# Narrower weight loads for the low products, and a later place for the first pair's far values

## The chip, the cores and the metric

The kernel runs on one core of a Trainium2 chip. The metric is the device time of one execution in microseconds (us); of a kernel that is run several times, the median counts.

## The reference: what is computed

One layer of a hybrid decoder on 1024 tokens of width 1024, all in float32:

```python
h = rmsnorm(x, mix_pre_norm[layer])
proj = h @ w_in[layer]
q_a, k_a, v_a, q_h, f_h, i_h, g_h = jnp.split(proj, splits, axis=-1)
...
attn = dilated_mixture_attention(q_a.reshape(ahead), k_a.reshape(ahead), v_a.reshape(ahead), slopes)
attn = rmsnorm(attn.reshape(B, S, ATTN_WIDTH), attn_out_norm[layer])
rec = hgrn2_recurrence(q_h, f_h, i_h, g_h, lower_bounds[layer], hgrn_out_norm[layer])
mixed = jnp.concatenate([attn, rec], axis=-1) @ w_out[layer]
x = x + rmsnorm(mixed, mix_post_norm[layer])
h = rmsnorm(x, mlp_pre_norm[layer])
ff = jnp.square(jax.nn.relu(h @ w_ff1[layer])) @ w_ff2[layer]
x = x + rmsnorm(ff, mlp_post_norm[layer])
```

The attention has 8 heads of 64 columns. Each query sees three sets of keys (a near window, every fourth token, every sixteenth token), and the three results are mixed by their softmax denominators. The recurrence (HGRN2) has 4 heads of 128 columns and is computed in blocks.

## The kernel before, in words

**Stages.** The core first does the 4 recurrence heads (`hgrn_core`), then the 8 attention heads in 4 pairs, then the output projection, then the feed-forward part, which is the longest (matrix products at line 2047 and lines 1602 to 1604). TensorE is fed in program order. Between the steps of a head a helper `fill` issues pieces of later projections from a queue, so that TensorE has work while the other engines prepare the next step. The projections of attention pairs 0 and 1 (`attn_proj(0)`, `attn_proj(1)`) are in this queue during the last recurrence head.

**High and low parts.** A product that must keep float32 precision is made of several products of rounded numbers: an operand is split into a high part (ScalarE rounds it, lines 86, 719, 993) and a low part (the rest, by VectorE or GpSimd). A projection is three products (`three_pass`, lines 90 to 92).

**Products with the values (`weigh`).** The values tile `v` holds for every block of 128 keys and each head of a pair 128 columns: 64 high columns and then 64 low columns. It is the stationary operand (its columns are the weight columns that are loaded), and the transposed probabilities are the moving operand. There are two products: the probabilities' high part (`pth`, `ptNh`, `ptFh`) and their low part (`ptl`, `ptNl`, `ptFl`). Both are accumulated into a PSUM tile of 128 rows, rows 0 to 63 for the high values and rows 64 to 127 for the low values, and later these halves are added (line 1062). Three kinds exist: D (line 1012; the diagonal part of a head, in two steps, 256 probabilities wide and at the last block 128 wide), F (line 1028, the far keys, 128 wide, three products for each of 4 classes), N (line 1034, the near window, 256 or 128 wide).

**Size-64 products of the recurrence.** At the end of each recurrence head 8 products of float32 numbers are made (line 583): the weights are 64 columns of `kt`, the moving operand is 64 columns of `qt`. Each appears in the profile as two matmuls, 64 of them in all 4 heads.

**Far values of pair 0.** The far products of pair 0 need the values in another order of rows. `values_turn` (line 756) makes the values tile and writes it to a buffer in HBM (`vd`, 8 DMAs at line 767); `far_load(0)` (line 665) makes two tiles `vf` in SBUF and fills them from there with 6 DMAs (line 672). All these DMAs are issued by SyncE (SP), which issues in program order. In the kernel before, `far_load(0)` is called at the end of the second `values_turn` of pair 0. Then follow on SP: the key copies of pair 0 (`kh`, `kl`; line 737: 4 and 4 DMAs from `hik` and `kf` for the first half of the tokens, 4 and 4 from `kp` for the second), with two weight loads (`raw`, line 107) among them; the first query copies of pair 1 (`q`, lines 798 and 799: 4 DMAs from `hiq` and `qf`); the second head's bias table (`bt`, line 855).

**What hangs on these copies.** `hiq`, `hik`, `qf`, `kf` share one pool of two buffers (`half`). VectorE makes `qf` out of the projection (line 793), ScalarE makes `hiq` from it (line 719), GpSimd makes the low part in place (line 720). The next `qf` needs a buffer whose copies by DMA have ended. Behind the second `qf` of pair 1 on VectorE stand the score steps of head 0 (line 901: add the bias and take the minimum). They empty the PSUM tiles `ps_D` and `ps_F`, of which there are two buffers, and the score products on TensorE (lines 896 and 897) and `px` (line 935) need these.

Of the kernel before, what the change touches and what calls it, by code (L numbers as in the profile page):

```python
# [17 lines left out]
P = 128  # L18
T = 1024
# [18 lines left out]
def hymba_layer(ctx, tc, x, w_in, w_out, w_ff1, w_ff2, g_pre, lb_logits, g_mix, g_post,  # L38
# [464 lines left out]
    def hgrn_core(h, after=None):  # L503
# [76 lines left out]
            fill(3500 if h < HH - 1 else (5300, 3100, 2000)[step])  # L580
        pl = bank("s", f"pl{h}_6")
        for n in range(NT):
            TE.matmul(pl[:64, n * 64:(n + 1) * 64], kt[:, n * P:n * P + 64], qt[:, n * P + 64:(n + 1) * P],
                      start=True, stop=True)
        S.activation(at[64:, :, 64:], at[64:, :, :64], AF.Copy)
        G.memset(at[64:, :, :64], 0.0)
# [75 lines left out]
    def key_blocks(ap, j0, j1):  # L662
        return ap.rearrange("p (r j i) -> p j r i", r=DIL, i=32)[:, j0:j1]

    def far_load(pr):
        fars[pr] = [slab("T", f"vf{pr}_{c}", F32R, (P, DIL, 2, 2, 64)) for c in range(2)]
        v2 = v_dram[pr].rearrange("(two odd) k c -> odd k two c", odd=2)
        for c in range(2):
            for odd in range(2):
                for c_, p0, k0, n in ((0, 0, 64 * odd, P), (1, 0, P - P * odd, 64), (1, 64, P - P * odd, 64)):  # L670
                    if c_ == c:
                        nc.sync.dma_start(out=f32(fars[pr][c][p0:p0 + n]).rearrange(
                            "p (two odd) h a d -> odd p two (h a d)", odd=2)[odd], in_=v2[odd, k0:k0 + n])
# [82 lines left out]
    def values_turn(tag="mm"):  # L756
        pr, vs, full, hf = turn_later.pop(0)
        pt = bank(tag, f"pvt{pr}{hf}")
        for j in range(4):
            TE.transpose(pt[:, j * P:(j + 1) * P], full[:, j * P:(j + 1) * P], ident)  # L760
        ptv = pt.rearrange("p (j h d) -> p j h d", j=4, h=2)
        dst = vs[:, hf * 4:hf * 4 + 4]
        S.activation(dst[:, :, :, 0, :], ptv, AF.Copy)
        V.tensor_tensor(out=dst[:, :, :, 1, :], in0=ptv, in1=f32(dst[:, :, :, 0, :]), op=ALU.subtract)
        b = slice(0, 4) if hf == 0 else slice(4, 6)
        for r in range(DIL):
            nc.sync.dma_start(out=v_dram[pr][r].rearrange("(n i) c -> i n c", i=32)[:, b],
                              in_=f32(vs[32 * r:32 * r + 32, b]).rearrange("p n h a d -> p n (h a d)"))
        if hf == 1 and pr == 0:
            far_load(0)  # L770

    def attn_proj(pr):
        stacks = [{}, {}]
# [4 lines left out]
        for hf in range(2):  # L778
# [17 lines left out]
            for i, (a, b) in enumerate(halves):  # L796
                c, d = halves[1 - i]
                nc.sync.dma_start(out=f32(stacks[i]["q"][a:b, sl]), in_=f32(hi[a:b]))
                nc.sync.dma_start(out=f32(stacks[i]["q"][c:d, sl]), in_=f32(lo[a:b]))
            yield 650.0  # L800
        wv = w_get(A0 + 3 * pr + 1, 0)
        vs = None
# [153 lines left out]
    def turn(hd, kind, g):  # L956
# [38 lines left out]
        if kind == "D" and g % 2 and hd // 2 < LASTP:  # L995
            V.reciprocal(st["rd"][:, g - 1:g + 1], st["dn"][:, g - 1:g + 1])

    def weigh(hd, kind, g):

        _, vs = pairs[hd // 2]  # L1000
# [4 lines left out]
        if kind == "D":  # L1005
# [3 lines left out]
            for j in range(nj):  # L1009
                c0 = P if j == nj - 1 else 0  # L1010
                for q in range(2):
                    TE.matmul(po[:, c0:256], v_of(vs, j), pt[q][:, j, c0:],  # L1012
                              start=j == 0 and q == 0, stop=j == nj - 1 and q == 1)
            ot = stats[hd]["D"][1] if g == 0 else stats[hd]["D"][3][:, :256]
            if hd // 2 == LASTP:
                S.activation(ot.rearrange("p (b i r) -> p b i r", b=2, r=DIL),
# [5 lines left out]
        if kind == "F":  # L1022
# [1 line left out]
                stats[hd]["po"] = bank("pv", f"pov{hd}_far")  # L1024
            po = stats[hd]["po"].rearrange("p (r m) -> p r m", r=DIL)
            for r in range(2 * g, 2 * g + 2):
                for n, (c, src) in enumerate(((0, pt[0][:, 0, r]), (0, pt[1][:, 0, r]), (1, pt[0][:, 1, r]))):
                    TE.matmul(po[:, r], v_of(fars[hd // 2][c], r), src, start=r == 0 and n == 0, stop=False,
                              skip_group_check=True)
            return None  # L1030
        po = stats[hd]["po"].rearrange("p (r m) -> p r m", r=DIL)
        for j, s0, n, c0 in (((3, 0, 1, 0), (4, 1, 2, 0)), ((5, 3, 2, 1), (6, 5, 2, 2), (7, 7, 1, 3)))[g]:
            for q in range(2):
                TE.matmul(po[:, :, c0 * 32:(c0 + n) * 32], v_of(vs, j),
                          pt[q][:, :, s0:s0 + n].rearrange("p r s i -> p r (s i)"),
                          start=False, stop=j == 7 and q == 1, skip_group_check=True)
        if g == 0:
# [1269 lines left out]
```

## Time and profile before

| | us |
|---|---|
| median of 3 runs | 1198.42 |
| lowest and highest | 1196.8 and 1199.7 |
| the profiled execution | 1198.21 |
| its span, from the first to the last instruction | 1196.4 |

The profile gives the busy time of each engine. PE stands for TensorE's matmuls, PEld for its weight loads, DVE for VectorE, ACT for ScalarE, POOL for GpSimd, SP for SyncE. In the timelines the columns are the start in us, the length in us, the engine, the line, the operation, its tiles (out<-in) and a count; in brackets at the end stand the idle time before it and what ended that. Matmuls are pipelined, so the length of one is more than its share of the time: how long one costs in a stream is read from the starts of the next. Rows of a form "128*128 128x256" give rows and columns of the array (the second number is the weight columns) and the size of the moving operand.

### The profile page before, as it was taken

To read this page: it belongs to the slowest core of one execution; us is meant where nothing else is said; L and a number is where in the kernel's file an instruction comes from. 1 tells how busy PE (TensorE), PEld (TensorE's weight loads), DVE (VectorE), ACT (ScalarE), POOL (GpSimd) and SP (SyncE) were. 2 spreads that over 40 slices of the span, in tenths; PEclk is the share of its full clock that TensorE was granted. 3 is DMA by queue.
4 is the path that set the end of the run, shared out by engine and by line. 5 is a ranking of instruction groups with operands and counts; after the bars stand their busy time and mean duration, and the time that the engine had idled before them with its cause. 6 is when DMAs were issued, how large, how long until landed. Compare 5 with 4: busy or idle time off the path is not lost.

```text
span 1196.4 us, 17598 instructions
## 1 busy us (share of the span) xinstructions
PE 1183.7 (99%) x6486; PEld 1008.3 (84%) x6486; DVE 839.9 (70%) x1427; ACT 548.6 (46%) x1082; POOL 296.0 (25%) x283
## 2 busy tenths in 40 slices
PE   9999999999999999999999999999999999999997
PEld 8898989878888888888888888888888888888886
DVE  5686969586666667675697666766677653578796
ACT  7633424333556667755653222222244544444562
POOL 0121212001111110152512776566540000000022
PEclk9999999999999999999999999999999999999999
DMA  5222323137454555372424565553687434533337
GB/s 219 71 68 85 98 84 110 42 104 188 95 134 104 142 145 143 93 236 91 173 98 159 175 215 208 178 182 143 218 324 271 162 104 143 174 90 104 107 105 281
DMA packets 90549, 175.49 MB, mean 147 GB/s; under 512 B 14944, under 2 KB 42464, under 8 KB 90464
## 3 DMA queue, kind: packets, MB, share of 16 engines
q1 hardware_dynamic: 90320, 174.37, 45.2%
q8 instruction: 51, 0.84, 0.3%
q14 instruction: 34, 0.28, 0.1%
q10 hardware_dynamic: 144, 0.00, 0.0%
HBM read 116.91 MB, written 47.99 MB: 138 GB/s over the span
## 4 chain that ended last, share of the span: by engine, by line
PE 75%; ACT 1%; DMA 1%; DVE 1%; issue 0%; SPq 0%; DVEq 0%; POOLq 0%; POOL 0%; ACTq 0%
PE f L2047 18%; PE f2s L2047 7%; PE pwo L92 2%; PE pwo L90 2%; PE pwo L91 2%; PE pm_ak L90 1%; PE pm_ak L92 1%; PE pm_ak L91 1%; PE pm_aq L90 1%; PE pov L1012 1%; PE pm_aq L92 1%; PE pm_av L90 1%; PE pm_aq L91 1%; PE pm_av L92 1%; PE pm_av L91 1%; PE pt_D L964 1%
## 5 line engine op out<-in xcount | busy, mean ns | idle before, releaser
L87 DVE TENSOR_TENSOR al<-ar,ah 128x1024 fp32r<-128x1024 f32 x56 | 70.7, 1262 | 81.3 <-ACT ah L86 78.9
L2047 PE MATMUL f<-bh,ah 128*128 128x512 f32 x320 | 124.5, 389 | 0.0
L2047 PE MATMUL f<-bl,ah 128*128 128x512 f32 x320 | 124.5, 389 | 0.0
L2047 PE MATMUL f<-bh,al 128*128 128x512 f32 x320 | 124.5, 389 | 0.0
L86 ACT ACTIVATE ah<-ar 128x1024 fp32r<-128x1024 f32 x56 | 59.2, 1056 | 85.8 <-DMA ar<-actd 84.0
L2047 PEld LDWEIGHTS f<-bh,ah 128*128 128x128 f32 x320 | 60.1, 188 | 12.6
L2047 PEld LDWEIGHTS f<-bl,ah 128*128 128x128 f32 x320 | 60.1, 188 | 12.5
L2047 PEld LDWEIGHTS f<-bh,al 128*128 128x128 f32 x320 | 60.1, 188 | 12.3
L2121 POOL TENSOR_SCALAR lbl<-ssq 128x1 f32<-128x1 f32 x4 | 4.1, 1013 | 244.1 <-ACT fd L2117 243.8
L1670 POOL TENSOR_TENSOR e<-x,e 128x512 f32<-128x512 f32 x14 | 21.6, 1540 | 131.9 <-DVE x L1621 124.7
L2047 PE MATMUL f2s<-bh,al 128*128 128x512 f32 (+1 forms) x128 | 48.9, 382 | 0.0
L2047 PE MATMUL f2s<-bl,ah 128*128 128x512 f32 (+1 forms) x128 | 48.9, 382 | 0.0
L2047 PE MATMUL f2s<-bh,ah 128*128 128x512 f32 (+1 forms) x128 | 48.9, 382 | 0.0
L703 POOL TENSOR_SCALAR tout<-traw 128x256 f32<-128x256 f32 x16 | 18.3, 1146 | 101.0 <-DMA traw<-in_bias_tab_dram 101.0
L87 DVE TENSOR_TENSOR bl<-br,bh 128x1024 fp32r<-128x1024 f32 x32 | 40.2, 1255 | 0.8 <-ACT bh L86 0.7
L2064 ACT ACTIVATE acc<-f 128x512 f32<-128x512 f32 x28 | 16.7, 598 | 49.2 <-PE f L2047 49.2
L751 POOL TENSOR_TENSOR kl<-kf,kh 64x512 fp32r<-64x512 f32 x12 | 16.2, 1350 | 79.2 <-ACT kh L750 79.2
L86 ACT ACTIVATE bh<-br 128x1024 fp32r<-128x1024 f32 x32 | 33.6, 1051 | 3.4 <-PE f L2047 2.3
L87 DVE TENSOR_TENSOR wl<-raw,wh 128x1024 fp32r<-128x1024 f32 x21 | 25.7, 1225 | 9.9 <-ACT wh L86 9.9
L90 PE MATMUL pwo<-woh,mt 128*128 128x512 f32 x80 | 32.2, 403 | 0.0
L92 PE MATMUL pwo<-woh,mt 128*128 128x512 f32 x80 | 31.3, 391 | 0.0
L91 PE MATMUL pwo<-wol,mt 128*128 128x512 f32 x80 | 31.2, 390 | 0.0
(1723 smaller groups left out, 3899.0 us busy)
## 6 DMA issues: line engine op xcount, KB each, us to landing
ar<-actd SPq DMA_DIRECT2D x56, 512.0 KB, 3.6
br<-in_w_ff_dram SPq DMA_DIRECT2D x16, 1024.0 KB, 5.9
raw<-in_w_in_dram SPq DMA_DIRECT2D x28, 512.0 KB, 3.9
w1r<-in_w_ff_dram SPq DMA_DIRECT2D x14, 1024.0 KB, 6.4
actd<-e SPq DMA_DIRECT2D x17, 768.0 KB, 4.2
actd<-e SPq DMA_DIRECT2D x11, 1024.0 KB, 4.1
xr<-in_x_dram SPq DMA_DIRECT2D x8, 512.0 KB, 8.1
raw<-in_w_out_dram SPq DMA_DIRECT2D x8, 512.0 KB, 3.9
```

Of the source, the lines that this page charges most:

```text
L86: S.activation(hi, src, AF.Copy)
L87: eng.tensor_tensor(out=lo, in0=src, in1=f32(hi), op=ALU.subtract)
L90: TE.matmul(dst, lhs[0], rhs[0], start=start, stop=False)
L91: TE.matmul(dst, lhs[0], rhs[1], start=False, stop=False)
L92: TE.matmul(dst, lhs[1], rhs[0], start=False, stop=stop)
L703: G.tensor_scalar(by_class(dst[:, part_ * w:(part_ + 1) * w]), in_blocks(raw[:, FAR * DIL:]), 8.0, None, op0=ALU.mult)
L751: G.tensor_tensor(out=kl[a:b], in0=src, in1=f32(kh[a:b]), op=ALU.subtract)
L964: TE.transpose(pt[:, j * P:(j + 1) * P], st["D"][b][:, j * P:(j + 1) * P], ident)
L1012: TE.matmul(po[:, c0:256], v_of(vs, j), pt[q][:, j, c0:], start=j == 0 and q == 0, stop=j == nj - 1 and q == 1)
L1670: eng[0].tensor_tensor(out=e1[:, 3], in0=a21, in1=e1[:, 2], op=ALU.add)
L2047: TE.matmul(pm, a[:, j, c], b[:, j, d], start=start and j == 0 and q == 0, stop=stop and j == 1 and q == 2, skip_group_check=True)
L2064: S.activation(acc_at(p, i), pm, AF.Copy)
```

## The change

Three things are changed.

First, `far_load(0)` is split. Its two tiles are still made at the end of the second `values_turn` of pair 0 (`far_room`). Its 6 DMAs are issued later, in `attn_proj(1)` behind the first 4 query copies.

Second, the products of the probabilities' low part with the values load only the first 66 columns of the values (the 64 high columns and 2 low ones) and write 66 rows of PSUM. The products of low probabilities with 62 of the 64 low value columns are thus left out. The products of the high part still have 128 columns.

Third, the size-64 products load 66 columns of `kt` instead of 64 and write 66 rows, of which 64 are read as before.

```diff
-            TE.matmul(pl[:64, n * 64:(n + 1) * 64], kt[:, n * P:n * P + 64], qt[:, n * P + 64:(n + 1) * P],
+            TE.matmul(pl[:66, n * 64:(n + 1) * 64], kt[:, n * P:n * P + 66], qt[:, n * P + 64:(n + 1) * P],
                       start=True, stop=True)
...
+    def far_room(pr):
+        fars[pr] = [slab("T", f"vf{pr}_{c}", F32R, (P, DIL, 2, 2, 64)) for c in range(2)]
+
     def far_load(pr):
-        fars[pr] = [slab("T", f"vf{pr}_{c}", F32R, (P, DIL, 2, 2, 64)) for c in range(2)]
+        if pr not in fars:
+            far_room(pr)
...
         if hf == 1 and pr == 0:
-            far_load(0)
+            far_room(0)
...
                 nc.sync.dma_start(out=f32(stacks[i]["q"][c:d, sl]), in_=f32(lo[a:b]))
+            if pr == 1 and hf == 0:
+                far_load(0)
...
+    LOW = 66
+    rows_of = (P, LOW)
...
-                    TE.matmul(po[:, c0:256], v_of(vs, j), pt[q][:, j, c0:],
-                              start=j == 0 and q == 0, stop=j == nj - 1 and q == 1)
+                    TE.matmul(po[:rows_of[q], c0:256], v_of(vs, j)[:, :rows_of[q]], pt[q][:, j, c0:],
+                              start=j == 0 and q == 0, stop=j == nj - 1 and q == 1, skip_group_check=True)
...
-                for n, (c, src) in enumerate(((0, pt[0][:, 0, r]), (0, pt[1][:, 0, r]), (1, pt[0][:, 1, r]))):
-                    TE.matmul(po[:, r], v_of(fars[hd // 2][c], r), src, start=r == 0 and n == 0, stop=False,
+                for n, (c, m, src) in enumerate(((0, P, pt[0][:, 0, r]), (0, LOW, pt[1][:, 0, r]), (1, P, pt[0][:, 1, r]))):
+                    TE.matmul(po[:m, r], v_of(fars[hd // 2][c], r)[:, :m], src, start=r == 0 and n == 0, stop=False,
                               skip_group_check=True)
...
-                TE.matmul(po[:, :, c0 * 32:(c0 + n) * 32], v_of(vs, j),
+                TE.matmul(po[:rows_of[q], :, c0 * 32:(c0 + n) * 32], v_of(vs, j)[:, :rows_of[q]],
```

The order of instructions is the same on VectorE, ScalarE and GpSimd. On SP only the 6 far loads move. SP before, at the place where they stood, behind the writes of the values (`vd`) and ahead of the first key copies of pair 0:

```order
L767 DMA vd_634<-v_2880 32x4x256 x4
L767 DMA vd_634<-v_2880 32x2x256 x4
L672 DMA vf_0_3065<-vd_634 128x2x256 x2
L672 DMA vf_1_3066<-vd_634 64x2x256 x4
L737 DMA kh_0_3001<-hik_3078 64x4x128 x2
L737 DMA kh_1_3003<-hik_3078 64x4x128 x2
```

SP in the changed kernel, at the same place:

```order
L771 DMA vd_634<-v_2880 32x4x256 x4
L771 DMA vd_634<-v_2880 32x2x256 x4
L741 DMA kh_0_3001<-hik_3072 64x4x128 x2
L741 DMA kh_1_3003<-hik_3072 64x4x128 x2
L741 DMA kl_0_3002<-kf_3070 64x4x128 x2
```

The key copies now follow the writes of the values at once. SP before, at the first query copies of pair 1 (`q_0` and `q_1` are the tiles of its two heads), behind the last key copy:

```order
L737 DMA kl_1_3004<-kp_3142 64x4x128 x2
L107 DMA raw_3187<-in_w_in_dram 128x1024
L798 DMA q_0_3215<-hiq_3219 64x512
L799 DMA q_0_3215<-qf_3217 64x512
L798 DMA q_1_3216<-hiq_3219 64x512
L799 DMA q_1_3216<-qf_3217 64x512
L855 DMA bt_3263<-tabd_639 128x704
```

SP in the changed kernel, at the same place:

```order
L741 DMA kl_1_3004<-kp_3136 64x4x128 x2
L107 DMA raw_3181<-in_w_in_dram 128x1024
L802 DMA q_0_3209<-hiq_3213 64x512
L803 DMA q_0_3209<-qf_3211 64x512
L802 DMA q_1_3210<-hiq_3213 64x512
L803 DMA q_1_3210<-qf_3211 64x512
L676 DMA vf_0_3065<-vd_634 128x2x256 x2
L676 DMA vf_1_3066<-vd_634 64x2x256 x4
L861 DMA bt_3263<-tabd_639 128x704
```

The far loads stand between these query copies and the bias table. On TensorE no instruction moves, only sizes differ. TensorE before, the first half of the far products of head 0 (the rows give weight columns x moving columns) and what follows:

```order
L1028 MATMUL pov_far<-ptFh_3437,vf_0_3065 128x128
L1028 MATMUL pov_far<-ptFl_3438,vf_0_3065 128x128
L1028 MATMUL pov_far<-ptFh_3437,vf_1_3066 128x128
L90 MATMUL pm_ak_3453<-hTh_91,wh_3400 128x512
L91 MATMUL pm_ak_3453<-hTl_92,wh_3400 128x512
```

TensorE in the changed kernel, at the same place:

```order
L1037 MATMUL pov_far<-ptFh_3437,vf_0_3065 128x128
L1037 MATMUL pov_far<-ptFl_3438,vf_0_3065 66x128
L1037 MATMUL pov_far<-ptFh_3437,vf_1_3066 128x128
L90 MATMUL pm_ak_3453<-hTh_91,wh_3400 128x512
L91 MATMUL pm_ak_3453<-hTl_92,wh_3400 128x512
```

Only the product with `ptFl` has 66 weight columns. (The three products stand there twice, for two classes; they are shown once.) The same holds of the products with `ptl` and `ptNl`.

## The prediction, made before the changed kernel had run

> **What bounds the kernel now.** I read the page first, then the waits of TensorE, then the timelines around its longest wait, then the timelines of the products that the change touches. The busy row of the page and the chain that ended last:
>
> ```profile
> PE 1183.7 (99%) x6486; PEld 1008.3 (84%) x6486; DVE 839.9 (70%) x1427; ACT 548.6 (46%) x1082; POOL 296.0 (25%) x283
> PE 75%; ACT 1%; DMA 1%; DVE 1%; issue 0%; SPq 0%; DVEq 0%; POOLq 0%; POOL 0%; ACTq 0%
> ```
>
> TensorE is the bound nearly everywhere, so what shortens its stream shortens the whole. It has one wait of more than a microsecond. The first two rows of the waits of TensorE that lie behind the start (total, times, longest):
>
> ```profile
> PE ps_F L896 <- DVE stat L901: 1.7, 1, 1.7
> ...
> PE ps_D L896 <- DVE stat L901: 0.7, 1, 0.7
> ```
>
> The timelines of TensorE and then of VectorE around the first wait:
>
> ```profile
> 299.35 0.39 PE L92 MATMUL pm_av<-hTh,wl 128*128 128x512 f32 x1
> 300.19 0.38 PE L935 MATMUL px<-pick,swap 128*128 128x4 f32 x2 [0.45 <-DVE stat L901]
> 302.23 0.53 PE L896 MATMUL ps_F<-kh,qc 128*128 128x192 f32 x1 [1.66 <-DVE stat L901]
> ```
>
> ```profile
> 296.90 0.60 DVE L645 SCALAR_TENSOR_TENSOR gate<-po,hrs,gate 128x128 f32<-128x128 f32 x2
> 298.83 0.69 DVE L793 TENSOR_TENSOR qf<-pm_aq,rrow 128x512 f32<-128x512 f32 x1 [1.33 <-DMA q<-hiq]
> ...
> 302.09 0.08 DVE L901 DVE_READ_ACCUMULATOR2_ANT stat<- 128x1 f32 x1
> ```
>
> TensorE waits for VectorE's score steps. VectorE was free at 297.50 but stood until 298.83, since the second `qf` of pair 1 needs a buffer that the first query copies were still reading. Those copies were late because of SP, whose timeline is this:
>
> ```profile
> 275.31 4.44 SPq L672 DMA_DIRECT2D vf<-vd  x6
> 279.80 2.60 SPq L737 DMA_DIRECT2D kh<-hik  x4
> 282.49 2.58 SPq L737 DMA_DIRECT2D kl<-kf  x4
> ...
> 288.56 3.07 SPq L737 DMA_DIRECT2D kl<-kp  x4
> 291.73 0.56 SPq L107 DMA_DIRECT2D raw<-in_w_in_dram  x1
> 292.39 0.48 SPq L798 DMA_DIRECT2D q<-hiq  x1
> ...
> 294.20 0.63 SPq L799 DMA_DIRECT2D q<-qf  x1
> 294.88 0.58 SPq L855 DMA_DIRECT2D bt<-tabd  x1
> ```
>
> SP issues without a pause from 275.31 to 295.46, and the far loads take 4.44 us at the head of that run. The wait has a second price, the clock. Busy times in three stretches of 3.40 us (PE, PEld, DVE, ACT, POOL, then the granted clock, the DMA share and GB/s), the third around the 0.7 us wait:
>
> ```profile
> 298.70:302.10 3.40, 1.42 (x7) 0.82 (x5) 2.26 (x10) 2.20 (x6) 1.27 (x1) 1.00 0.18 43
> 302.10:305.50 3.40, 3.27 (x12) 2.98 (x13) 2.50 (x13) 0.49 (x1) 0.00 (x0) 0.51 0.50 116
> 452.00:455.40 3.40, 2.66 (x16) 2.19 (x15) 3.34 (x10) 2.42 (x8) 0.05 (x1) 1.00 0.57 131
> ```
>
> Right behind the wait TensorE runs at 0.51 of its clock for 3.40 us; the 0.7 us wait costs no clock.
>
> **The far loads: what the move removes.** SP then starts the key copies at 275.31 and is 4.44 us earlier with each of them. The first query copies need their data:
>
> ```profile
> 285.84 0.69 DVE L793 TENSOR_TENSOR qf<-pm_aq,rrow 128x512 f32<-128x512 f32 x1 [0.15 <-PE pm_aq L92]
> 287.00 0.63 ACT L719 ACTIVATE hiq<-qf 128x512 fp32r<-128x512 f32 x1 [5.41 <-DMA kl<-kf]
> 287.76 1.29 POOL L720 TENSOR_TENSOR qf<-qf,hiq 128x512 fp32r<-128x512 f32 x1 [11.68 <-ACT hiq L719]
> ```
>
> ScalarE's wait there is for the key copies too; with these 4.44 us earlier it starts when `qf` is ready, 286.53, and GpSimd ends near 288.6. SP would be free at 292.39 - 4.44 = 287.95. So the last of the four query copies goes out near 290 instead of 294.20. That copy is the one VectorE waited for, and it had landed by 298.83, 4.63 us after its issue; with the same delay it lands near 294.6, before VectorE is free at 297.50. The 1.33 us go. What is late next is VectorE's own work: `qf`, the scores, ScalarE's exponentials between them. Its last step before the `ps_F` product, which ended at 302.17, keeps its distance and ends at 300.84. TensorE is ready for `px` at 299.35 + 0.23 = 299.58, with the 0.23 that a 512-wide product takes in the stream (rows further down), and the scores that `px` waits for are then done. Adding 0.14 for `px` (an estimate; it is small either way), it waits for `ps_F` from 299.72 to 300.90: about 1.2 us instead of two waits that add to 2.5 us with the gap between them.
>
> The idle time of 1.2 us is nearer to the 0.7 us that kept the clock than to 2.5 us that lost it, so I take the clock as kept. That is worth 3.40 x (1 - 0.51) = 1.67 us, less the 0.13 us of the stretch in which TensorE was idle anyway: 1.6 us. The sum for the stall is 1.33 + 1.6 = 2.9 us; 1.3 if the clock falls all the same, 0 if another transfer takes the place of this one.
>
> The Trainium skill weighs on this term, "TensorE: Matmul & The Clock Gate", section "Why this matters for your kernels": it asks for no idle gaps of over about 3 us between bursts, since a full window of idle halves the clock. By that rule the 2.5 us here should have cost no clock, and the stall would be worth 1.3 us and the whole 1.6 us less. The row differs (0.51 behind a gap below 3 us), and the row decides.
>
> What the loads cost at their new place: 4.44 us of SP between the query copies and the bias table. They would run from about 290.5 to 295 and the table goes out at about its old 294.88. The far tiles are first read at 314 (the `ptFl` row below), so they have almost 20 us. I cost the new place at nothing; the cover is that slack, and were it gone, TensorE would wait at line 1028 for whatever is missing.
>
> **The low products.** The loads and products at the end of a D step of head 0:
>
> ```profile
> 310.89 0.19 PEld L1012 LDWEIGHTS pov<-ptl,v 128*128 128x128 f32 x1
> 311.00 0.19 PEld L90 LDWEIGHTS pm_ak<-hTh,wh 128*128 128x128 f32 x1
> 311.11 0.19 PEld L91 LDWEIGHTS pm_ak<-hTl,wh 128*128 128x128 f32 x1
> ```
>
> ```profile
> 310.76 0.28 PE L1012 MATMUL pov<-ptl,v 128*128 128x256 f32 x1
> 310.88 0.22 PE L1012 MATMUL pov<-pth,v 128*128 128x128 f32 x1
> 310.95 0.28 PE L1012 MATMUL pov<-ptl,v 128*128 128x128 f32 x1
> ```
>
> Loads of 128 columns follow each other every 0.11 us. A 256-wide product takes 0.12 us (310.76 to 310.88), so the next load hides behind it. A 128-wide product takes about 0.06 (310.88 to 310.95), so the next load shows. The size-64 products have the price of a narrow load, in one grouped row and the products around it:
>
> ```profile
> 96.38 1.01 PEld L583 LDWEIGHTS pl<-qt,kt 128*64 128x64 f32 x16 [0.35 <-issue]
> ```
>
> ```profile
> 95.83 0.39 PE L91 MATMUL pm_q<-hTl,wh 128*128 128x512 f32 x1
> 96.06 0.39 PE L92 MATMUL pm_q<-hTh,wl 128*128 128x512 f32 x1
> 96.38 1.15 PE L583 MATMUL pl<-qt,kt 128*64 128x64 f32 x16
> 97.45 0.50 PE L90 MATMUL pm_q<-hTh,wh 128*128 128x512 f32 x1
> 97.79 0.39 PE L91 MATMUL pm_q<-hTl,wh 128*128 128x512 f32 x1
> ```
>
> A single such load lasts about 0.14 us, so 16 loads that end after 1.01 us follow each other every (1.01 - 0.14) / 15 = 0.058 us. No load of 66 columns is in the trace. Its bounds are 0.058 (64 columns) and 0.11 (128); I take 0.060, since 66 is next to 64 and 0.058 is close to half of 0.11. Where a low load stands under a 128-wide product, 0.11 becomes 0.06, 0.05 us saved; under a 256-wide one nothing is saved. How many there are, from the groups of the three lines:
>
> ```profile
> L1012 PE MATMUL pov<-ptl,v x48: 272/280/385, 305.3 to 492.6; 128*128 128x256 f32 x32, 128*128 128x128 f32 x16
> L1028 PE MATMUL pov_far<-ptFl,vf x32: 272/273/277, 314.0 to 497.8; 128*128 128x128 f32 x32
> L1034 PE MATMUL pov_far<-ptNl,v x40: 272/279/388, 320.1 to 501.7; 128*128 128x256 f32 x24, 128*128 128x128 f32 x16
> ```
>
> The low product comes right behind the high one of the same width, so 16 + 32 + 16 = 64 low loads stand under a 128-wide product: 64 x 0.05 = 3.2 us. VectorE is on average less loaded than TensorE there, but some steps already wait for it (the 0.7 us at 453.8), so I take 3.0. If the load takes as long as 128 columns, it is 0.
>
> **The size-64 products.** From the start of the 512-wide product before them (96.06) to that of the second one after (97.79) pass 1.73 us. Two 512-wide products at 0.23 (95.83 to 96.06) and 16 at 0.058 need 0.46 + 0.93 = 1.39. The excess of 0.34 is paid where the array goes from 128 to 64 weight columns and back; 0.05 of it is a 128-column load that shows behind a short product, as at 311.00. If 66 columns count as the full width, 0.29 goes, less 16 x 0.002 = 0.03 for two more columns: 0.26 a head, 1.0 us for four. The other bound: if a load of 66 columns costs 0.11, each head loses 16 x 0.053 - 0.29 = 0.56, which makes 2.2 us of loss.
>
> **The sum.** 2.9 + 3.0 + 1.0 = 6.9 us. The profiled execution had 1198.21 us (span 1196.4), 0.2 below the median of 1198.42. So the profiled execution would go to 1191.3, and the median to **1191.5 us**.
>
> **The rivals.**
>
> *Loads in steps of 32 columns.* If 66 columns load like 96, a load takes 0.058 + (0.11 - 0.058) / 2 = 0.084. The low products then save 64 x 0.026 = 1.7, each head of size-64 products loses 16 x 0.026 - 0.29 = 0.13 (0.5 in all). Sum 2.9 + 1.7 - 0.5 = 4.1: 1194.3. Nothing in the trace lies between 64 and 128 columns.
>
> *Loads like 128 columns.* Sum 2.9 + 0 - 2.2 = 0.7: 1197.7. Against it: 64 columns take half of 128.
>
> *The stall stays in part.* The DMA engines are well loaded in this stretch, and VectorE may wait for another copy, or the clock may fall at 1.2 us of idle too. With the clock lost 6.9 - 1.6 = 5.3: 1193.1; with the whole stall kept 4.0: 1194.4.
>
> *Slower: each change of width drains the array.* The 0.34 us excess could be the price of any change in the number of weight columns, not of the 64. The change puts 48 + 32 + 40 = 120 low products of 66 columns between products of 128, so 120 x 0.3 = 36 us, and the time would be 1198.4 - 2.9 + 36 = 1231.5. It turns the sign as soon as one such change costs more than 2.9 / 120 = 0.024 us beyond what it saves. For it: the only place in the trace with another width has this excess. Against it: those are halves of the array, and 66 columns are no half. The Trainium skill, "TensorEngine Tiling (Array Packing)", section "Key Properties", says that a change of tiling mode drains the array, and lists modes of 128, 64 and 32 columns only; no run here shows a width between.
>
> **How the numbers follow.** The forecast has 0.62; steps of 32 columns 0.12; part of the stall kept 0.16; loads like 128 columns 0.05; slower 0.04; the rest is for what I don't see. About 0.2% (2.4 us) is what a measurement of this kernel can tell from no change. Faster than 1196.0 are the first three, 0.89 with a part of the rest cut off; the same is mostly the fourth, 0.07; slower 0.04. The forecast's own range is 1190 to 1193. The range of 8 in 10 goes down to 1189.8 (all 64 loads at 0.05, and the rest of the wait smaller than I take it) and up to 1195.0, past the partial cases.
>
> **What would show it.** Right: in the profile after, SP's first query copies of pair 1 go out at 288 to 290; the wait of `qf` for a DMA is gone; `ps_F` waits about 1.2 us; the granted clock behind it stays at 1.00; low loads are followed by the next product after 0.06 us instead of 0.11 where the width is 128; the size-64 products take about 0.26 us less from the product before to the second after, and without the idle 0.35 before their first load. Wrong: a low load that keeps 0.11 or takes 0.084; an idle time before low loads; a new wait at line 1028 for the far tiles; the clock at a half near 302.

## The result, and the profile after

The changed kernel takes 1192.06 us (median of 5 runs, 1191.88 to 1192.31) against 1198.42 for the kernel before (median of 5 runs, 1196.8 to 1199.7). The ratio is 0.9948 with a 95% interval of 0.9937 to 0.9959, so it is faster by 4.9 to 7.5 us. The profiled execution took 1191.88 us with a span of 1189.9 us. The forecast was 1191.5, with a range of 1189.8 to 1195.0.

The order of the matmuls is the same in both kernels, 6486 of them. So the gain can be placed: take the start of the same matmul in both traces, and watch how the difference (after minus before) changes from stage to stage.

| stage | difference at its start and end, us | change |
|---|---|---|
| start of the kernel (the first input by DMA) | 0 to +0.28 | +0.28 |
| the four recurrence heads | +0.28 to -0.87 | -1.15, of it -0.25 or -0.26 at each of the four size-64 places |
| around the wait for `ps_F` | -0.87 to -3.81 | -2.94 |
| the rest of the attention | -3.81 to -6.46 | -2.66 |
| output projection and feed-forward | -6.46 to -6.51 | -0.05 |

The 0.28 at the start comes before anything that the change touches. Some 0.1 of the heads' gain lies outside the four places, at a product of line 764 near 262 us. Now the lines that answer to those shown of before. The busy row of the page:

```profile
PE 1178.0 (99%) x6486; PEld 1004.0 (84%) x6486; DVE 840.3 (71%) x1427; ACT 548.8 (46%) x1082; POOL 297.3 (25%) x283
```

TensorE is still the bound. The waits of TensorE, the two that the prediction spoke of:

```profile
PE ps_F L902 <- DVE stat L907: 1.0, 1, 1.0
PE ps_D L902 <- DVE stat L907: 0.8, 1, 0.8
```

The first has gone from 1.7 to 1.0, and the 0.5 for `px` ahead of it is gone. The second is as it was. SP's timeline shows why:

```profile
274.55 2.65 SPq L741 DMA_DIRECT2D kh<-hik  x4
...
286.15 0.55 SPq L107 DMA_DIRECT2D raw<-in_w_in_dram  x1
286.81 0.48 SPq L802 DMA_DIRECT2D q<-hiq  x1
...
290.62 0.59 SPq L803 DMA_DIRECT2D q<-qf  x1
291.26 4.65 SPq L676 DMA_DIRECT2D vf<-vd  x6
295.95 0.59 SPq L861 DMA_DIRECT2D bt<-tabd  x1
```

The key copies go first. The last query copy is issued at 290.62 instead of 294.20, and the six far loads follow it. The bias table leaves 1.07 later than before (295.95 for 294.88), and no wait for it or for the far tiles stands among TensorE's. VectorE and then TensorE around the wait:

```profile
296.03 0.60 DVE L645 SCALAR_TENSOR_TENSOR gate<-po,hrs,gate 128x128 f32<-128x128 f32 x2
296.55 0.68 DVE L797 TENSOR_TENSOR qf<-pm_aq,rrow 128x512 f32<-128x512 f32 x1
```

```profile
298.71 0.28 PE L941 MATMUL px<-pick,swap 128*128 128x4 f32 x2
299.94 0.36 PE L902 MATMUL ps_F<-kh,qc 128*128 128x192 f32 x1 [0.95 <-DVE stat L907]
```

The row of `qf` has no bracket any more: the 1.33 us wait for a DMA is gone. Nor has that of the two `px`; only `ps_F` waits, 0.95 us. The busy times of the engines, one stretch around the wait and one behind it (the same columns as before, the granted clock behind POOL):

```profile
299.00:302.40 3.40, 2.46 (x17) 2.24 (x18) 3.10 (x17) 1.30 (x5) 0.31 (x1) 1.00 0.65 154
302.40:305.80 3.40, 3.40 (x21) 2.92 (x20) 2.62 (x8) 2.95 (x9) 0.00 (x0) 1.00 0.08 11
```

The clock stays at 1.00. What the lost clock had cost is seen in the products behind the wait. Before (TensorE's timeline), the first low product that is 128 wide with its neighbours:

```profile
305.54 0.23 PE L1012 MATMUL pov<-pth,v 128*128 128x128 f32 x1
305.61 0.27 PE L1012 MATMUL pov<-ptl,v 128*128 128x128 f32 x1
305.72 0.45 PE L90 MATMUL pm_av<-hTh,wh 128*128 128x512 f32 x1
```

The same place after:

```profile
301.73 0.22 PE L1021 MATMUL pov<-pth,v 128*128 128x128 f32 x1
301.79 0.22 PE L1021 MATMUL pov<-ptl,v 128*66 128x128 f32 x1
301.85 0.45 PE L90 MATMUL pm_av<-hTh,wh 128*128 128x512 f32 x1
```

From the start of `ps_F` to that of the high product took 305.54 - 302.23 = 3.31 us before and takes 301.73 - 299.94 = 1.79 now: 1.52 us for the clock. The other 1.42 of the 2.94 are waiting time. The last two rows show the low product's gain: the next product starts 0.06 us after it, where it was 0.11.

The size-64 place of the first head after, weight loads and then matmuls:

```profile
96.33 1.20 PEld L583 LDWEIGHTS pl<-qt,kt 128*66 128x66 f32 x16
```

```profile
96.33 0.39 PE L92 MATMUL pm_q<-hTh,wl 128*128 128x512 f32 x1
96.55 1.12 PE L583 MATMUL pl<-qt,kt 128*66 128x64 f32 x16
97.48 0.48 PE L90 MATMUL pm_q<-hTh,wh 128*128 128x512 f32 x1
97.79 0.39 PE L91 MATMUL pm_q<-hTl,wh 128*128 128x512 f32 x1
```

No idle time stands before the loads (before, 0.35 us did). From the product before to the second after pass 97.79 - 96.33 = 1.46 us instead of 1.73, by the rounded starts 0.27 less, and 0.26 in the differences above.

### The profile page after: what moved, and what is told of

It is laid out like the page before. It is cut to its first block, busy times and chain, and to the rows that moved or that the text cites. A ratio compares the mean times of both kernels' runs of the same rounds, so it can differ in the third digit from the quotient of the medians.

```text
span 1189.9 us, 17595 instructions
## 1 busy us (share of the span) xinstructions
PE 1178.0 (99%) x6486; PEld 1004.0 (84%) x6486; DVE 840.3 (71%) x1427; ACT 548.8 (46%) x1082; POOL 297.3 (25%) x283
## 4 chain that ended last, share of the span: by engine, by line
PE 74%; ACT 1%; issue 1%; DMA 1%; DVE 1%; POOL 0%; DVEq 0%; POOLq 0%; SPq 0%; ACTq 0%
PE f L2056 18%; PE f2s L2056 7%; PE pwo L92 2%; PE pwo L90 2%; PE pwo L91 2%; PE pm_ak L90 1%; PE pm_ak L92 1%; PE pm_ak L91 1%; PE pm_aq L90 1%; PE pm_aq L92 1%; PE pm_aq L91 1%; PE pm_av L90 1%; PE pm_av L92 1%; PE pm_av L91 1%; PE pov L1021 1%
```

## The experiments

The theory was that of the prediction: three terms that don't touch each other (the far loads take SP's time, the low loads show under 128-wide products, 64 columns cost a drain that 66 don't), and a half clock as a part of the stall's price. Its rivals: the stall's wait is all there is to it; the low products gain by something other than the width of their loads; any change of width drains. The times of before beside the experiments are 1198.25 (27 runs, e1 to e4), 1198.26 (16 runs, e5 to e8) and 1197.82 (12 runs, e9 to e12).

### Each part alone

**e1_far_only.** The changed kernel with the low products on 128 columns and the size-64 products on 64.

```diff
-    LOW = 66
+    LOW = P
...
-            TE.matmul(pl[:66, n * 64:(n + 1) * 64], kt[:, n * P:n * P + 66], qt[:, n * P + 64:(n + 1) * P],
+            TE.matmul(pl[:64, n * 64:(n + 1) * 64], kt[:, n * P:n * P + 64], qt[:, n * P + 64:(n + 1) * P],
```

> Only the far loads are moved; all products keep their 128 and 64 weight columns. Theory (the loads held up the query copies, and the wait that followed cost the clock as well): 2.9 us less than before, 1195.5 us; the wait of qf for a DMA is gone, ps_F waits about 1 us, and no stretch near 302 us has half the clock. Rival (the three parts help only together, because the shorter products free TensorE to reach the wait earlier or later): less than 1.5 us. Rival (the clock falls at 1 us of idle too): 1.3 us less, 1197.1.

Measured: 1195.95 us (11 runs), ratio 0.9981 (0.9973 to 0.9990), a gain of 2.3 us in the medians where 2.9 was expected. In the trace the difference to before goes from +0.40 to -2.53 at the stall, 2.93 us; elsewhere it moves by 0.2 at most. TensorE at the wait:

```profile
301.22 0.36 PE L902 MATMUL ps_F<-kh,qc 128*128 128x192 f32 x1 [0.95 <-DVE stat L907]
```

The same 0.95 as in the whole change. So the move of the far loads alone makes the stall's term. That less than 2.9 arrives at the end is seen in the trace too: this execution had lost 0.40 us ahead of the stall (0.18 at the start of the kernel, 0.22 at a product of line 764 near 262 us), so the two profiled spans differ by 2.4 (1196.4 and 1194.0).

The kernel before doesn't lose the clock in every run: of its 27 runs the 8 with a mean granted clock of 0.999 lie at 1196.06 to 1197.11 us, the 19 with 0.996 to 0.998 at 1197.62 to 1200.91.

**e2_low_only.** The far loads at their old place, the size-64 products on 64 columns, only `LOW = 66`.

```diff
-            far_room(0)
+            far_load(0)
...
-            if pr == 1 and hf == 0:
-                far_load(0)
...
-            TE.matmul(pl[:66, n * 64:(n + 1) * 64], kt[:, n * P:n * P + 66], qt[:, n * P + 64:(n + 1) * P],
+            TE.matmul(pl[:64, n * 64:(n + 1) * 64], kt[:, n * P:n * P + 64], qt[:, n * P + 64:(n + 1) * P],
```

> Only the low products have 66 weight columns; the far loads stand where they stood and the size-64 products have 64 columns. Theory (64 low loads that show under 128-wide products cost 0.06 us instead of 0.11): between 2.7 us (what the changed kernel shows in this stretch) and 3.2 us less, 1195.2 to 1195.7 us, all of it between the first and the last product with the values, and the stall near 302 us as before. Rival (the other engines take the gain back once the far loads are in the way again): under 1 us.

Measured: 1194.90 us (11 runs, 1193.45 to 1197.47), ratio 0.9972 (0.9963 to 0.9981), 0.3 below what was expected. In the trace the difference to before goes from +0.13 ahead of the stall to -2.25 at the end of the attention, 2.4 us; the stall itself is 0.24 longer here, and behind it the low products gain 2.6. The half clock is there as before. The stretch that holds both waits (0.59 and 1.76 us) and the next, cut where the clock changes:

```profile
300.28:303.69 3.41, 1.48 (x10) 1.36 (x11) 2.04 (x13) 1.93 (x7) 1.27 (x1) 1.00 0.33 76
303.69:307.11 3.42, 3.42 (x14) 2.93 (x13) 1.63 (x8) 1.81 (x4) 0.00 (x0) 0.50 0.34 80
```

**e3_size64_only.** The far loads at their old place and `LOW = P` (the lines of the two diffs above), only the size-64 products on 66 columns.

> Only the size-64 products of the recurrence have 66 weight columns. Theory (the array pays 0.29 us for going to 64 columns and back): 4 x 0.26 = 1.0 us less, 1197.4 us, in four steps of 0.26 at the four places, and no idle time before the first of these loads. Rival (the steps are given back at VectorE's next wait): 0 to 0.5 us.

Measured: 1197.50 us (11 runs), ratio 0.9999 (0.9990 to 1.0008). The time can't tell a gain of 1 us from none: the interval reaches 1.2 us below. The trace can. Its difference to before has a step of 0.26 at each of the four places (+0.11 to -0.15 at the first, -0.87 to -1.13 at the last). This execution has the stall too, with waits of 0.67 and 1.66 us, but no half clock:

```profile
299.74:303.15 3.41, 1.79 (x12) 1.66 (x13) 2.59 (x15) 1.69 (x6) 0.97 (x1) 1.00 0.51 117
303.15:306.56 3.41, 3.41 (x22) 2.94 (x21) 2.30 (x5) 2.67 (x7) 0.00 (x0) 1.00 0.16 39
```

Its stall stage is 1.27 us shorter than that of before, though its first wait is 0.22 longer: what differs in its favour is the clock.

### The clock

**e5_warm.** The kernel before, with five spare products (512 wide, into a bank that nothing reads) ahead of the waiting `ps_F`. Waits and copies stay as they are; only TensorE is busy for longer in the gap.

```diff
+        if s == 2:
+            spare = bank("t", "spare")
+            for k in range(5):
+                TE.matmul(spare, part(hT, k % 4, 0)[0][:, :P], part(hT, k % 4, 0)[0], start=True, stop=True)
         for d, kind, g in looks[:1]:
             look(hd + d, kind, g)
```

> The kernel before with five added 512-wide products of values that lie ready, into a spare PSUM tile that nobody reads, right ahead of the ps_F product that waits 1.66 us. They remove no wait; they need 5 x 0.23 = 1.15 us and fit into the idle time. Theory (half of the stall's price is the clock, which falls because TensorE was idle too long): the wait still ends where it ended, but the clock stays at 1.00 behind it, 1.6 us less than before, 1196.8 us. Rival (the clock fell for another reason, and the price is the wait alone): no change, 1198.4 us.

Measured: 1196.20 us (11 runs), ratio 0.9987 (0.9978 to 0.9995), a gain of 0.6 to 2.6 us with more work done (1196.8 was expected). TensorE at the wait, and two stretches that take in the wait and what follows:

```profile
299.50 0.39 PE L935 MATMUL px<-pick,swap 128*128 128x4 f32 x2 [0.51 <-DVE stat L901]
299.75 1.42 PE L1360 MATMUL spare<-hTh 128*128 128x512 f32 x5
301.55 0.35 PE L896 MATMUL ps_F<-kh,qc 128*128 128x192 f32 x1 [0.39 <-DVE stat L901]
```

```profile
297.77:301.18 3.41, 2.88 (x13) 1.75 (x11) 2.02 (x8) 2.20 (x6) 1.29 (x1) 1.00 0.16 41
301.18:304.59 3.41, 3.04 (x21) 2.79 (x22) 2.82 (x15) 1.04 (x3) 0.00 (x0) 1.00 0.54 123
```

From `px` to `ps_F` pass 2.05 us, as in before (300.19 to 302.23), so the wait itself hasn't moved. The clock is kept (1.00 in both stretches), and the products behind it take 1.5 us less. The clock is a price of its own, as the prediction had it.

### The width of the loads

**e4_low64.** The changed kernel with the low products on 64 columns (none of the low values).

```diff
-    LOW = 66
+    LOW = 64
```

> As the changed kernel, but the low products have 64 weight columns instead of 66 (the two low columns that 66 takes are left out as well). Theory (going from 128 to 64 columns and back costs 0.29 us, whatever the product): the runs of 128, 64, 128 columns pay it at each of the 120 low products, up to 120 x 0.29 = 35 us more than with 66 columns, about 1227 us; somewhat less where a 256-wide product covers a part. Rival (the price lies in the change from rounded to full float32 products at the size-64 place, not in the columns): as with 66 columns, 1192 us.

Measured: 1191.76 us (5 runs), ratio 0.9946 (0.9934 to 0.9958), where a drain at each product would have given some 1227. The theory fell here. The first low product that is 128 wide, on TensorE:

```profile
302.05 0.23 PE L1021 MATMUL pov<-ptl,v 128*64 128x128 f32 x1
302.11 0.44 PE L90 MATMUL pm_av<-hTh,wh 128*128 128x512 f32 x1
```

0.06 us and no idle time: 64 columns cost nothing by themselves. The time is that of the rival, but its reason, a price for changing from rounded to full float32, is still to be tried. What differs between these products and the size-64 ones is the kind of number. The low products are of rounded float32 and have one matmul each, the size-64 products are of full float32 and have two. That became the new theory: the drain belongs to full float32 products on 64 columns.

**e10_low64_full and e11_low66_full.** The low products as full float32 products, on 64 and on 66 columns. The lines of N and F change in the same way.

```diff
+    as_of = (lambda x: x, f32)
...
-                    TE.matmul(po[:rows_of[q], c0:256], v_of(vs, j)[:, :rows_of[q]], pt[q][:, j, c0:],
+                    TE.matmul(po[:rows_of[q], c0:256], as_of[q](v_of(vs, j)[:, :rows_of[q]]), as_of[q](pt[q][:, j, c0:]),
```

> The changed kernel with the low products as full float32 products (two matmuls each) on 64 weight columns. To be read against the next kernel, which has 66 columns and is otherwise the same; both are slower than the changed kernel, since 120 products become 240 matmuls (some 120 x 0.1 to 0.4 = 12 to 50 us). Theory A, the 0.29 us at the size-64 place is the price of a full float32 product on 64 columns between products on 128: each of the 120 low products stands alone between products on 128 columns, so this kernel is up to 120 x 0.29 = 35 us slower than the one with 66 columns, with an idle time of about 0.3 us before each such load. Theory B, the 0.29 us belongs to something else at that place: the two kernels differ by less than 1 us.

> The changed kernel with the low products as full float32 products (two matmuls each) on 66 weight columns. Theory A: no idle time before these loads, and up to 35 us faster than the same products on 64 columns. Theory B: the same time as on 64 columns within 1 us. If changing from rounded to full float32 products has a price of its own, it shows here too, as an idle time before the low loads.

Measured: 1253.71 us on 64 columns (4 runs, ratio 1.0465, 1.0451 to 1.0480) and 1214.02 on 66 (4 runs, ratio 1.0132, 1.0118 to 1.0146). They differ by 39.7 us, 0.33 for each of the 120 low products. On 64 columns, the weight loads of one high and one low product:

```profile
308.22 0.19 PEld L1022 LDWEIGHTS pov<-pth,v 128*128 128x128 f32 x1 [0.39 <-issue]
308.53 0.19 PEld L1022 LDWEIGHTS pov<-ptl,v 128*64 128x64 f32 x2
309.11 0.19 PEld L1022 LDWEIGHTS pov<-pth,v 128*128 128x128 f32 x1 [0.39 <-issue]
```

On 66 columns:

```profile
306.17 0.19 PEld L1022 LDWEIGHTS pov<-pth,v 128*128 128x128 f32 x1
306.39 0.26 PEld L1022 LDWEIGHTS pov<-ptl,v 128*66 128x66 f32 x2
306.72 0.19 PEld L1022 LDWEIGHTS pov<-pth,v 128*128 128x128 f32 x1
```

A pair takes 0.89 us (308.22 to 309.11) on 64 columns and 0.55 (306.17 to 306.72) on 66. In the first, the weight engine stands for 0.39 us behind each low product, ahead of the load of 128 columns, with nothing to wait for that the profile shows (the expectation had the idle time ahead of the low load). In the second there is no idle time. So a full float32 product on 64 columns pays what this document calls a drain, and the same product on 66 does not. The Trainium skill, "TensorEngine Tiling (Array Packing)", section "Key Properties", says that changing the tiling mode drains TensorE. These two traces agree for full float32 (0.34 us for each pair); with rounded numbers on 64 columns (e4) nothing of it shows, which the section does not tell apart.

The rival of e4 falls here: the change from rounded to full float32 is the same in both kernels, and on 66 columns it shows no idle time. It isn't free, though. The products at the same place on 66 columns, on TensorE:

```profile
305.84 0.28 PE L1022 MATMUL pov<-pth,v 128*128 128x256 f32 x1
305.96 0.59 PE L1022 MATMUL pov<-ptl,v 128*66 128x256 f32 x2
306.20 0.47 PE L1022 MATMUL pov<-pth,v 128*128 128x256 f32 x1
306.50 0.60 PE L1022 MATMUL pov<-ptl,v 128*66 128x256 f32 x2
```

The high product behind a rounded product takes 0.12 us (305.84 to 305.96), the one behind a full float32 product 0.30 (306.20 to 306.50). Of the 22.0 us by which e11 is slower than the changed kernel, 12 lie in the low products, which have a second matmul, and 10 in the high products, which are the same in both kernels. What makes these 10 is open. The kernel on 64 columns changes between the kinds just as often, so its 0.33 come on top of that.

**e9_size128.** The changed kernel with the size-64 products on all 128 columns of `kt`.

```diff
-            TE.matmul(pl[:66, n * 64:(n + 1) * 64], kt[:, n * P:n * P + 66], qt[:, n * P + 64:(n + 1) * P],
+            TE.matmul(pl[:, n * 64:(n + 1) * 64], kt[:, n * P:n * P + P], qt[:, n * P + 64:(n + 1) * P],
```

> The changed kernel with the size-64 products on 128 weight columns (all of kt). My theory: a load costs by its columns, 0.060 us at 66 and 0.111 at 128, and the array does not drain at 128, so 64 matmuls x 0.051 = 3.3 us more than the changed kernel: 1195.3, and the 0.26 us of each place's drain does not come back as an idle time of <-issue. Rival: the loads hide behind the products (a full float32 product of 64 columns has two matmuls, and each could last longer than its load): then the time stays within 0.5 us of 1192.1.

Measured: 1194.90 us (8 runs), ratio 0.9975 (0.9965 to 0.9986), 2.8 us above the changed kernel, and 3.1 in the traces (3.3 was expected). The weight loads of the first head:

```profile
96.22 1.98 PEld L583 LDWEIGHTS pl<-qt,kt 128*128 128x128 f32 x16
98.12 0.19 PEld L90 LDWEIGHTS pm_q<-hTh,wh 128*128 128x128 f32 x1
```

No idle time, so 128 columns don't drain either, but each load costs 0.11 us instead of 0.060. For these products 66 is better than 128 and than 64.

**e7_low_wide.** 66 columns only under the products that are 256 wide; those that are 128 wide have 128 columns. The line of D is shown, F and N change alike.

```diff
-                    TE.matmul(po[:rows_of[q], c0:256], v_of(vs, j)[:, :rows_of[q]], pt[q][:, j, c0:],
+                    m = P if c0 else rows_of[q]
+                    TE.matmul(po[:m, c0:256], v_of(vs, j)[:, :m], pt[q][:, j, c0:],
```

> The changed kernel with 66 weight columns only in the 56 low products that are 256 wide (of which 8 stand under a mixed run); the 64 that are 128 wide have 128 columns again. Theory (a load under a 256-wide product is hidden whatever its size): the whole gain of the low products is lost, 2.7 us more than the changed kernel, 1194.8 us. Rival (a narrower product is itself shorter or leaves the array sooner, whatever its moving width): about half is kept, 1193.4 us.

Measured: 1194.04 us (6 runs), ratio 0.9970 (0.9957 to 0.9982), 0.8 below what was expected, of which 0.3 lie at the start of the kernel. In the trace the attention gains 0.2 us (-4.06 to -4.24) where the changed kernel gains 2.66. The gain lies under the 128-wide products; a narrower load under the 256-wide ones is worth next to nothing (0.2 us for all 56), as the prediction had it.

**e8_low96.** The changed kernel with `LOW = 96`.

> The changed kernel with 96 weight columns in the low products instead of 66. Theory (a load's price goes by its columns, 0.058 us for 64 and 0.11 for 128, in a straight line): 0.084 us, so 64 x 0.024 = 1.5 us are lost, 1193.6 us. Rival (any load below the full width takes the short time): as with 66, 1192.1 us. Rival (above some count the full time is taken): 1194.8 us.

Measured: 1193.05 us (5 runs), ratio 0.9964 (0.9952 to 0.9977). The attention gains 1.5 us (-3.83 to -5.34), 1.15 less than with 66 columns, where a loss of 1.5 was expected; the steps at the 64 products themselves add to 1.72 us instead of 3.09. The weight loads at the first 128-wide low product:

```profile
301.72 0.16 PEld L1021 LDWEIGHTS pov<-ptl,v 128*96 128x96 f32 x1
301.80 0.19 PEld L90 LDWEIGHTS pm_av<-hTh,wh 128*128 128x128 f32 x1
```

A load of 96 columns takes 0.08 us, between 0.060 for 66 and 0.11 for 128. The price goes by columns.

### The wait that was left

**e6_fill_early.** The changed kernel with one projection piece (three products, 0.69 us) moved ahead of `ps_F`, and another that was meant for the `ps_D` that waits near 447.

```diff
+        if s in (2, 40):
+            fill(0.0, True)
         for d, kind, g in looks[:1]:
             look(hd + d, kind, g)
...
-    UNITS = ((2, 3, 2, 3,
+    UNITS = ((2, 3, 1, 3,
...
-             (3, 3, 3, 4, 2, 3, 3, 2), (3, 3, 3, 2, 1, 2, 2, 2),
+             (3, 3, 3, 4, 2, 3, 3, 2), (2, 3, 3, 2, 1, 2, 2, 2),
```

> The changed kernel with one piece of a projection (three 512-wide products, 0.69 us) taken from behind its two longest remaining waits, 0.95 us for ps_F near 300 us and 0.78 us for ps_D near 448 us, and put ahead of each. Nothing is added. Theory (these waits are set by VectorE's chain, which doesn't hang on the moved piece, so work put into them is free): up to 0.69 us at each, 1.0 to 1.4 us less than the changed kernel, 1190.7 to 1191.1 us. Rival (TensorE waits again a little later, since the piece is missing there): the same as the changed kernel, 1192.1 us.

Measured: 1191.38 us (5 runs, 1191.31 to 1191.57), ratio 0.9948 (0.9935 to 0.9960): 0.7 us below the changed kernel, half of what was expected. The wait for `ps_F` is filled but for 0.13 us: the product ahead of it ends at 300.04, and `ps_F` starts at 300.17. The second piece was misplaced. It stands ahead of a `ps_D` product near 424, which doesn't wait, and the one near 447 still waits 0.77 us. So that wait was not tried, and half of what was expected is missing.

**e12_both.** The changed kernel with `LOW = 64` and only the piece ahead of `ps_F`.

```diff
-    LOW = 66
+    LOW = 64
...
+        if s == 2:
+            fill(0.0, True)
         for d, kind, g in looks[:1]:
             look(hd + d, kind, g)
...
-    UNITS = ((2, 3, 2, 3,
+    UNITS = ((2, 3, 1, 3,
```

> The changed kernel with the low products on 64 weight columns (1191.76 where tried alone, 0.3 below the changed kernel) and with one projection piece moved ahead of the waiting ps_F product (0.7 below, where two pieces were moved and only this one gained). If the two add: 1192.06 - 0.3 - 0.7 = 1191.1. Rival: the 0.3 was scatter of runs, and the time stays at 1191.4.

Measured: 1190.37 us (5 runs, 1190.36 to 1190.83), ratio 0.9937 (0.9924 to 0.9949), the best of all kernels here and 0.7 below what was expected. Against the changed kernel its trace is 1.4 us shorter: 0.8 at the wait, 0.3 at the start of the kernel (ahead of all that differs), 0.3 in the rest of the attention. What is left of the wait for `ps_F` is 0.15 us.

That 64 columns are better than 66 in the low products is not settled: the two kernels that have only this between them (e4 and the changed kernel) lie 0.3 us apart.

## Why the prediction was right, point by point

**The far loads: 2.9 forecast, 2.94 measured.** The steps held one after the other. The first query copy goes out at 286.81, earlier than the 288 to 290 of the forecast, since this stage as a whole comes 0.9 us earlier; the last one goes out at 290.62 (forecast near 290), `qf` no longer waits, VectorE's own work is late next. The wait that is left was sized at 1.2 us and is 0.95. The two parts, forecast as 1.33 and 1.6, are 1.42 and 1.52. (The forecast's 1.67 less 0.13 is 1.54 and not 1.6; the sum of 2.9 is the same with it.) The new place of the loads cost nothing, as forecast. e1 shows that this part alone makes the term, and e5 that the clock is a part of it.

The reason given for the clock was too simple. The prediction compared idle times (0.7 us kept the clock, 2.5 lost it) and put the threshold between them. e3 kept the clock with 0.67 + 1.66 us of waiting, more than the 0.45 + 1.66 that lost it in before. What fits all traces is the time that TensorE was busy in a fixed stretch of 3.41 us. In each of the 14 traces the changes of the granted clock lie at whole multiples of 3.413 us from each other (in the kernel before at 5.18, 302.14, 305.55 and 1193.01 us), and these give the borders of all other stretches of that trace. By them TensorE was busy for 1.39 us in the stretch ahead of the fall in before (298.73 to 302.14; the row from 298.70 has 1.42) and for 1.48 in e2. The clock stayed behind 1.79 us in e3, where a border at 299.74 parts the two waits, behind 2.70 in the changed kernel and 2.88 in e5, and behind 1.70 in a stretch near the end of e12 (1180.53 to 1183.94). Two falls are few for a threshold; it lies between 1.48 and 1.70 as far as these traces go. By this the forecast of a kept clock had more room than its reason gave it: a single wait of 1.2 us leaves at least 2.2 us of a stretch busy.

The Trainium skill, "TensorE: Matmul & The Clock Gate", section "What's actually happening", says that the window is free-running and 3413 ns long. The traces agree with that. Borders that fall differently from run to run would make the same waits cost the clock in some runs only, and that fits the two groups of runs of before (e1). It is a part of its scatter of 4.9 us at most: the 19 runs at the lower mean clock alone lie up to 3.3 us apart, which no trace here explains.

**The low products: 3.0 forecast, 2.66 measured.** The mechanism was right: each 128-wide low product is followed after 0.06 us instead of 0.11, the steps in the differences are 0.044 to 0.056 at nearly all of the 64 places and add to 3.09 us (3.2 in the forecast), and e7 and e8 show that the gain lies under these products and goes by columns. The size was off by 0.3: waits take back some 0.6 where 0.2 was set aside. One place is the first `pt_N` in the last pair's far part, TensorE's timeline after:

```profile
492.35 0.40 PE L92 MATMUL pwe<-wh,emt 128*128 128x512 f32 x1
492.82 0.66 PE L979 MATMUL pt_N<-ident,pn 128*128 128x128 f32 x4
```

A 512-wide product takes 0.23, so TensorE stood here for 0.24 us until ScalarE had the exponentials ready. The others, 0.04 to 0.1 each, lie between 439 and 464 around the `ps_D` wait.

**The size-64 products: 1.0 forecast, 4 x 0.26 = 1.0 measured.** The number was right, and so was the idle time that goes. The step that failed is the reason, that the excess "is paid where the array goes from 128 to 64 weight columns and back". e4 has 120 such changes and pays nothing. e10 and e11 show what it is: a full float32 product on 64 columns costs 0.33 us between products on 128, on 66 columns it doesn't. That the forecast still came out lies in the bounds: they were taken from the size-64 rows themselves. That 66 columns would escape the price was a guess from their being no half of the array, and no row stood behind it.

The prediction also took line 583 for the only place in the trace with another width than 128. It is not: line 535 makes products on 64 columns, 384 matmuls in 12 runs of 32, two matmuls for each product as at line 583. One run in the changed kernel, with its neighbours on TensorE:

```profile
78.00 0.28 PE L92 MATMUL pig<-wig1h,hTl 128*128 128x256 f32 x1
78.21 1.54 PE L535 MATMUL pl<-qs,kt 128*64 128x96 f32 x32
79.69 0.39 PE L90 MATMUL pig<-wig1h,hTh 128*128 128x256 f32 x1
79.91 0.28 PE L91 MATMUL pig<-wig1l,hTh 128*128 128x256 f32 x1
```

From 78.00 to 79.91 pass 1.91 us. Two 256-wide products need 0.24, and 32 matmuls that start every 0.042 us ((1.54 - 0.25) / 31, with 0.25 for the length of one) need 1.34. The excess is 0.33, that of the size-64 place before the change. It stands at all 12 places, in three of them with a wait for another engine on top, in both kernels. So the change took the price away at 4 places of 16; 12 x 0.28 = 3.4 us is an estimate of what is left, with 0.05 of each excess kept for the 128-column load that shows. No run here tries another width there, and two spare columns don't fit as they stand: half of these products write the last 64 rows of their tile.

**The rivals.** Slower by a drain at every change of width fell with the result: the loads of 66 columns show no idle time. Its mechanism does exist, for full float32 numbers and 64 columns, and e10 is what it looks like. Loads like 128 columns and steps of 32 columns fell too (66 columns take 0.060, 96 take 0.08, 128 take 0.11). The stall stays in part fell: the 0.95 us that are left are less than the 1.2 in the forecast itself, and the clock is kept.

**The sum.** 6.9 us forecast; 2.94 + 2.66 + 1.02 = 6.6 measured, and 0.28 lost at the start of the kernel, which belongs to no part of the change. That the median came within 0.6 us of the forecast is in part luck, since such starts differ by up to 0.8 us between these traces (e5 and e6). The profiled execution went down by 6.3 (1198.21 to 1191.88), the median by 6.4.

## What to carry to other kernels

A transfer that is not needed soon should not stand in a queue ahead of one that is: count back from the first reader of each, and move the one with 20 us of slack. When an engine's wait ends, read the granted clock behind it before you price the wait, since here the clock cost as much as the wait. A narrower weight load pays only where the product ahead of it is shorter than the load; and of full float32 products, avoid 64 columns between products on 128, two spare columns are cheaper than the drain. Before you call a place the only one of its kind, list all products by their width.

## What the runs showed of the hardware

- A full float32 product on 64 weight columns between products on 128 costs 0.33 us more than the same product on 66 (e10 against e11), and a run of 32 of them has an excess of 0.33 as well (line 535). The same width with rounded numbers costs nothing (e4: 1191.76 us, where 120 drains would have been some 35 us more), and full float32 products on 66 or 128 columns show no such idle time (e11, e9).
- Full float32 products set singly between rounded ones have a price on 66 columns too: the rounded 256-wide product behind one takes 0.30 us instead of 0.12 (e11, cause open).
- The price of a weight load that shows goes by columns: 0.060 us at 66, 0.08 at 96, 0.11 at 128.
- The granted clock changes only at borders 3.413 us apart (all 14 traces). A stretch between two borders in which TensorE was busy for 1.39 or 1.48 us was followed by one at half clock (before, e2); with 1.70 or more it was not (e12, e3). Neither of the two was idle as a whole.
- The same stall doesn't cost the clock in every run: e3 kept it with longer waits than those that lost it in the kernel before.
